# A hybrid linear-attention and softmax-attention encoder: order of the key products, and of the first weight blocks and last input blocks of a feed-forward stage

## The chip, the cores and the metric

One core of one Trainium2 chip runs the whole program in one launch. A core has five engines with an instruction stream each: TensorE (PE: matrix products and transposes, results in PSUM), VectorE (DVE), ScalarE (ACT), GpSimd (POOL) and SyncE (SP, which only starts transfers). They meet through semaphores. Transfers are started from the queue of SP, ACT or POOL and carried out by 16 DMA engines. The metric is the device time of the launch in microseconds (us), the median of several runs. A profile is a trace of one execution; its span runs from the first to the last instruction.

## The reference, cut to what matters

The model has two layers over 528 tokens (512 and 16 learned meta tokens), width 1024, all in float32. A layer is: half a feed-forward step, a mixer, half a feed-forward step.

```python
for l in range(DEPTH):
    h = h + 0.5 * swiglu(rmsnorm(h, g[l, 0]), w_gate[l, 0], w_up[l, 0], w_down[l, 0])
    h = h + mixer(rmsnorm(h, g[l, 1]), ...)
    h = h + 0.5 * swiglu(rmsnorm(h, g[l, 2]), w_gate[l, 1], w_up[l, 1], w_down[l, 1])
return rmsnorm(h, final_norm)[:, N_META:]

def swiglu(x, w_gate, w_up, w_down):                 # hidden width 2816
    return (silu(x @ w_gate) * (x @ w_up)) @ w_down
```

One branch of the mixer is gated linear attention with 4 heads, in chunks and in both directions. For a chunk with decay logs summed up along it (`bcum`, and `btot` at its end) it needs three scaled copies of queries and keys:

```python
q_dec = qc * exp(bcum)            # queries, decayed from the chunk's start
k_inv = kc * exp(-bcum)           # keys for the products inside the chunk
k_end = kc * exp(btot - bcum)     # "end keys": what a key is worth at the chunk's end
att      = where(mask, q_dec @ k_inv.T, 0);   o_intra = att @ vc
kv_chunk = k_end.T @ vc                       # what the chunk adds to the state
```

`k_end.T @ vc` contracts over tokens, so the end keys must be transposed on the chip first. The other branch is softmax attention; the change doesn't touch it.

## The kernel before, in words

**Layout and precision.** Activations lie transposed: 128 channels on the partitions, 528 tokens along the row, eight such chunks for the width. Every large product is done as three products of a rounded high part (`hi`) and the rest (`lo`): hi*hi, hi*lo, lo*hi. A weight tile is 128 x 1024 floats, 512 KB: fetched by SP into `raw` (3 buffers), copied to `whi` by ACT (line 238), and the rest put into `wlo` by DVE (line 239), 4 buffers each. `Weights.use(j)` makes `hi` and `lo` for loads up to j+3 and starts fetches up to j+5 (`AHEAD_MADE`, `AHEAD_FETCHED`).

**A planner sets the order.** The code is traced once. A planner then gives each engine its fixed instruction stream: of the instructions that are ready by its own estimates of durations it takes the one that comes first in the code (`tc.high_priority()` puts some ahead), and it may move a later instruction ahead of one that isn't ready yet. On the chip each stream runs strictly in order, so an instruction that isn't ready in truth holds up all that stands behind it on its engine, also on the queues of SP and POOL.

**Feed-forward stages.** There are four: (0,0), (0,1), (1,0), (1,1), for layer and position. The gate and up products are done for pairs of 128-column blocks (11 pairs a stage) by seven products in place of eight (Strassen-Winograd) on 2 x 2 blocks: the weight is cut in blocks 11, 12, 21, 22, the input in `b11` to `b22` (two channel chunks by two halves of the tokens). Products 1, 2 and 4 take the blocks 11, 12, 22 as fetched. The other four take sums of blocks:

- product 7 takes s3 = 21 - 11 (pool `wsa`, ACT negates 11 on line 189, POOL adds 21)
- product 6 takes s2 = 22 + s3 (pool `wsb`, SP fetches 22, POOL adds s3)
- product 5 takes s1 = 21 + 22 (pool `wsb`, SP fetches 21, POOL adds 22)
- product 3 takes s4 = s2 - 12 (pool `wsa`, ACT negates 12 on line 189, POOL adds s2)

The additions are transfers that add to their target, started from POOL's queue (line 194). `wsa` has 3 buffers and `wsb` has 2. `sums` (lines 196 to 211) is called by `make` just after a block's `hi` and `lo`: for product 1 it does s3 and s2, for product 2 it does s1 and s4.

The input side holds seven combinations for each of four channel pairs, in one tile `xc` with seven slots, `hi` and `lo` (`pair`, lines 475 to 502): slots 0 and 1 are b11 and b21 for products 1 and 2, slots 2 to 5 hold sums for 5, 6, 7, 4, slot 6 is -b22 for product 3. The chunk before the stage calls `chunk_of_pair(c)` as each of the eight chunks of `h` is finished; the sum of squares for the norm is gathered by the way (line 450 on ACT, line 454 on DVE). The norm's factor `rs` itself is only applied later, on the results.

**Openings.** The first products of stages (0,1), (1,0) and (1,1) run while the stage before ends. The order in the code is: products 1 and 2 of pair 0 together (`two_products`, line 580, three channel pairs first and then the last one), products 1 and 2 of pair 1, 6 and 5 of pair 0, 7, 4 and 3 of pair 0, 6 and 5 of pair 1 and so on (line 597). Below, "6 of pair 1" means such a product. Results go through copies of PSUM (`snap`, line 608).

**Linear attention.** `gla_pair` runs per layer for two pairs of heads, each with two directions d, so there are 8 passes. A pass makes the decay logs on ACT (lines 724 to 726), sums them along chunks on DVE (727, 731), subtracts middle and end values (737 to 742), exponentiates on ACT (746 to 755) and forms `qp` on DVE (757), `kp`, the keys inside the chunk, on POOL (758), and `ke`, the end keys, on DVE (760). PE transposes `ke` (764, 765), DVE copies the result out (767, 769). Between these steps PE works on projections of the mixer (line 404, through `project`).

Of the kernel before, what the change touches and what calls it, by code (L numbers as in the profile page):

```python
# [158 lines left out]
class Weights:  # L159
# [35 lines left out]

    def sums(self, f, i, product, w):


        got = self.summed
        if product == "1":  # L200
            s3 = self.negative(f, i, "s3", w)
            self.add(s3, self.dram(f, i, "21"))
            s2 = self.block(f, i, "22", self.short, "wsb")
            self.add(s2, s3)
            got[f, i, "7"], got[f, i, "6"] = s3, s2
        else:
            s1 = self.block(f, i, "21", self.short, "wsb")
            self.add(s1, self.dram(f, i, "22"))
            s4 = self.negative(f, i, "s4", w)
            self.add(s4, got[f, i, "6"])  # L210
            got[f, i, "5"], got[f, i, "3"] = s1, s4

    def fetch(self, upto):

        while self.fetched < min(upto, len(self.loads)):
            load = self.loads[self.fetched]
            if isinstance(load, int):
                w = self.raw.tile([P, SLAB], F32, tag="raw", name=f"raw{load}")
                self.nc.sync.dma_start(w, self.wts[load])
                self.raws[self.fetched] = w  # L220
            elif load[2] in DIRECT:
                self.raws[self.fetched] = self.block(*load[:2], DIRECT[load[2]])
            self.fetched += 1

    def make(self, upto):
        nc = self.nc
        while self.made < min(upto, len(self.loads)):
# [15 lines left out]
            if not isinstance(load, int) and load[2] in ("1", "2"):  # L243
                self.sums(*load, w)
# [28 lines left out]
def build(tc, ctx, xt, wts, win, par, w2, const, umask, out):  # L273
# [10 lines left out]
    slots = {n: pool("s_" + n, b) for n, b in dict(g=16, t=6, rs=2).items()}  # L284
# [151 lines left out]
    class Norm:  # L436
# [38 lines left out]
        def pair(self, j):  # L475
# [18 lines left out]
            S.activation(hi[:, 6], b22, AF.Copy, scale=-1.0)  # L494
            V.scalar_tensor_tensor(lo[:, 6], b22, -1.0, hi[:, 6].bitcast(F32), ALU.mult, ALU.subtract)
# [6 lines left out]
            parts(slice(4, 6), v2(t34))  # L502

# [36 lines left out]
    def ffn(l, f, norm, done, following):  # L540
# [25 lines left out]
        def two_products(p, names):  # L566
# [132 lines left out]
    def gla_pair(l, p, lr, w2t, sr, qa, ka, va, n_out):  # L699
# [17 lines left out]
        for d in range(2):  # L717
# [22 lines left out]
            V.tensor_tensor(a[:, MB], src[:, MB], mm_, ALU.subtract)  # L740
            V.tensor_tensor(blk(ct_), blk(src), tot, ALU.subtract)
            V.tensor_copy(ct_[:, MB], a[:, MB])
            r16 = 1.0 / 16.0
            qp, kp = slot("p"), slot("p")
            if d == 0:
# [3 lines left out]
                S.activation(ct_, ct_, AF.Exp, scale=-r16)  # L749
                ein, eq, ek, eend = c, a, g, ct_  # L750
            else:
                S.activation(c, a, AF.Exp, scale=-r16)
                S.activation(a, a, AF.Exp, scale=r16)
                S.activation(ct_, ct_, AF.Exp, scale=-r16)
                S.activation(g, g, AF.Exp, scale=r16)
                ein, eq, ek, eend = ct_, c, a, g
            V.tensor_tensor(qp[:, :n_out], qa, eq[:, :n_out], ALU.mult)
            G.tensor_tensor(kp, ka, ek, ALU.mult)
            ke = slot("p")
            V.tensor_tensor(ke, ka, eend, ALU.mult)  # L760

            tp = pair()
            for b, bs, _ in blocks:
                TE.transpose(tp[:, 0, bs], ke[:, bs], ident)
            TE.transpose(tp[:META, 1, :P], ke[:, MB], ident)
# [260 lines left out]
    def block_pools():  # L1026
        pools = open_pools("left", wsa=3, wsb=2)
# [248 lines left out]
```

## Time and profile before

| what | value |
|---|---|
| runs | 2263.21 us median of 3 (2260.45 to 2268.38) |
| the profiled execution's own time | 2263.49 us |
| its span | 2261.6 us |
| PE busy | 2204.5 us, 97% of the span |
| DVE, ACT, POOL busy | 1527.2, 1218.3, 164.7 us |
| PE waiting for `ke` at line 764 | 12.5 us in 8 waits |
| additive transfers from POOL | 4 kinds, 43 of each, 512 KB |

On PE the stages lie in the span as follows: (0,0) up to 376 us, mixer of layer 0 to 789, (0,1) to 1148, (1,0) to 1519, mixer of layer 1 to 1900, (1,1) to the end. The page of the profile names each group by line, engine and operation, output and inputs by the program's names: `w<-win` is a block fetched from memory by SP, or added to a `wsb` buffer by POOL; `s<-w` is a `wsa` buffer, either written by ACT from the block it negates (line 189) or raised by POOL by the sum s2 (line 194); `w<-s` is s2 raised by s3; `s<-win` is s3 raised by block 21.

### The profile page before, as it was taken

How to read it: one execution, taken by the hardware profiler on the slowest of the kernel's cores; microseconds unless marked ns; L12 is line 12 of the kernel's file. 1: busy time of each engine (PE TensorE's matmuls, PEld its weight loads, DVE VectorE, ACT ScalarE, POOL GpSimd, SP SyncE). 2: the span in 40 equal slices, each digit the busy share in tenths (PEclk: the TensorE clock that was granted, in tenths of full speed). 3: DMA queues.
4: the chain of work that ended last, by engine and by line, in shares of the span. 5: the costliest groups of instructions: out<-in, count | busy, mean ns of one | idle time of the engine just before them, and what ended most of it. 6: DMA issues, size and time to landing. Idle time of an engine off the chain costs nothing. (4 is left out here: it accounts for less than half of the span.)

```text
span 2261.6 us, 39885 instructions
## 1 busy us (share of the span) xinstructions
PE 2204.5 (97%) x16538; PEld 2102.9 (93%) x16538; DVE 1527.2 (68%) x2397; ACT 1218.3 (54%) x1824; POOL 164.7 (7%) x184
## 2 busy tenths in 40 slices
PE   8999999999999999999979999999999999999998
PEld 8999999989999999999979999998888888989897
DVE  7657567577876666565676565575789767756565
ACT  8536355344784564453565363454557836636354
POOL 1011000000000010101011010100000000101010
PEclk9999999999999999999999999999999999999999
DMA  8778463211113485867658585732121135869661
GB/s 239 188 177 212 134 168 108 75 57 57 48 38 113 124 203 154 197 174 173 180 139 207 139 217 149 178 105 87 56 68 54 47 121 152 215 155 225 156 181 66
DMA packets 87542, 312.85 MB, mean 138 GB/s; under 512 B 9664, under 2 KB 11840, under 8 KB 87360
## 3 DMA queue, kind: packets, MB, share of 16 engines
q1 hardware_dynamic: 60816, 217.67, 28.6%
q0 software_dynamic: 24768, 90.19, 22.5%
q8 instruction: 130, 2.13, 0.4%
q10 hardware_dynamic: 1776, 2.43, 0.3%
q14 instruction: 52, 0.43, 0.1%
HBM read 263.07 MB, written 2.10 MB: 117 GB/s over the span
## 5 line engine op out<-in xcount | busy, mean ns | idle before, releaser
L597 PE MATMUL ss<-xc,whi 128*128 128x264 f32 (+1 forms) x4720 | 865.1, 285 | 16.9 <-ACT whi L238 9.5
L597 PEld LDWEIGHTS ss<-xc,whi 128*128 128x128 f32 x4720 | 734.7, 189 | 19.7 <-ACT whi L238 10.3
L597 PE MATMUL ss<-xc,wlo 128*128 128x264 f32 (+1 forms) x2360 | 671.4, 285 | 5.1 <-DVE wlo L239 5.1
L404 PE MATMUL ss<-g,whi 128*128 128x264 f32 (+1 forms) x2620 | 482.8, 300 | 0.0
L597 PEld LDWEIGHTS ss<-xc,wlo 128*128 128x128 f32 x2360 | 446.8, 189 | 6.4 <-DVE wlo L239 6.3
L404 PEld LDWEIGHTS ss<-g,whi 128*128 128x128 f32 x2620 | 380.6, 188 | 15.7
L404 PE MATMUL mm<-x,whi 128*128 128x264 f32 (+1 forms) x1712 | 385.8, 315 | 0.0
L238 ACT CAST whi<-w 128x1024 fp32r<-128x1024 f32 (+1 forms) x220 | 230.0, 1046 | 266.2 <-PE ss L404 116.1
L239 DVE TENSOR_TENSOR wlo<-w,whi 128x1024 fp32r<-128x1024 f32 (+1 forms) x220 | 266.6, 1218 | 116.1 <-ACT whi L238 114.8
L238 ACT CAST whi<-raw 128x1024 fp32r<-128x1024 f32 x190 | 199.2, 1048 | 260.2 <-PE ss L597 89.8
L239 DVE TENSOR_TENSOR wlo<-raw,whi 128x1024 fp32r<-128x1024 f32 x190 | 232.1, 1222 | 105.8 <-ACT whi L238 104.8
L404 PE MATMUL ss<-g,wlo 128*128 128x264 f32 (+1 forms) x1310 | 302.2, 300 | 0.0
L404 PEld LDWEIGHTS mm<-x,whi 128*128 128x128 f32 x1712 | 281.2, 190 | 15.3 <-DVE x L393 0.2
L404 PE MATMUL mm<-x,wlo 128*128 128x264 f32 (+1 forms) x856 | 265.2, 314 | 0.0
L404 PEld LDWEIGHTS ss<-g,wlo 128*128 128x128 f32 x1310 | 209.2, 188 | 8.3
L239 DVE TENSOR_TENSOR wlo<-s,whi 128x1024 fp32r<-128x1024 f32 x86 | 105.1, 1222 | 95.7 <-ACT whi L238 95.6
L238 ACT CAST whi<-s 128x1024 fp32r<-128x1024 f32 x86 | 90.3, 1050 | 146.9 <-PE ss L597 128.3
L404 PEld LDWEIGHTS mm<-x,wlo 128*128 128x128 f32 x856 | 161.2, 190 | 7.6
L527 DVE SCALAR_TENSOR_TENSOR t<-ss,rs 128x528 f32<-128x528 f32 (+1 forms) x93 | 64.6, 700 | 126.4 <-PE ss L404 126.3
L189 ACT ACTIVATE s<-w 128x1024 f32<-128x1024 f32 x86 | 91.2, 1060 | 81.7 <-DMA w<-win 46.5
L194 POOL DMA_DIRECT2D w<-win x43 | 37.8, 880 | 599.3 <-DVE wlo L239 222.3
L393 DVE TENSOR_TENSOR g<-c,g 128x528 fp32r<-128x528 f32 (+1 forms) x88 | 61.5, 699 | 22.6 <-ACT g L392 22.6
(280 smaller groups left out, 2829.6 us busy)
## 6 DMA issues: line engine op xcount, KB each, us to landing
w<-win SPq DMA_DIRECT2D x218, 512.0 KB, 4.7
raw<-wts SPq DMA_DIRECT2D x190, 512.0 KB, 3.3
w<-win POOLq DMA_DIRECT2D x43, 512.0 KB, 6.8
s<-win POOLq DMA_DIRECT2D x43, 512.0 KB, 6.7
w<-s POOLq DMA_DIRECT2D x43, 512.0 KB, 5.9
s<-w POOLq DMA_DIRECT2D x43, 512.0 KB, 7.0
h<-xt SPq DMA_DIRECT2D x3, 528.0 KB, 7.6
out<-h SPq DMA_DIRECT2D x2, 512.0 KB, 2.9
```

What stands on the lines that cost most here:

```text
L189: self.nc.scalar.activation(t, w, AF.Copy, scale=-1.0)
L194: self.nc.gpsimd.dma_start(t, src, accum_op=ALU.add)
L238: nc.scalar.copy(hi[:, cs], w[:, cs])
L239: nc.vector.tensor_tensor(lo[:, cs], w[:, cs], hi[:, cs].bitcast(F32), ALU.subtract)
L393: V.tensor_tensor(lo, src, hi.bitcast(F32), ALU.subtract)
L404: TE.matmul(acc.half[i][:width], lhs, rhs[:, acc.spans[i]], start=first, stop=last)
L527: V.scalar_tensor_tensor(cut(dst[rows]), pv[rows], -0.5 * f, cut(rs[rows]), ALU.mult, ALU.mult)
L597: TE.matmul(acc[:, j], a[:, j, k], b[:, at], start=bool(begin and k == 0 and i == 0), stop=k == len(x) - 1 and i == 2, skip_group_check=no ...
```

## The change

In the linear attention the end keys and their transposes come first in a pass, under high priority, directly from the decay sums; for d = 0 only the difference that they need is formed, and two small steps fall away. `kp` is formed on VectorE instead of GpSimd.

In the openings, for pair 0 of the three later stages, s3, s2 and s1 are called where block 11 is fetched, and s4 where block 12 is fetched, both two loads earlier in the code than before. For pair 1, s3 and the negation for s4 stay at products 1 and 2, but the fetch and addition of s2, and the addition of s2 to s4, are called after `hi` and `lo` of product 6 of pair 0, and s1 after those of product 5 of pair 0. `wsa` gets a fourth buffer. To make room for it `rs` has one buffer instead of two, and the decay weights (`w2`) live in a pool of the mixer.

The last of the four input pairs is written in two parts: `early` fills slots 0 and 1 straight from `h`; `late`, called after the matrix products of `two_products`, fills slots 2 to 6 and adds the squares of the last two chunks. In every pair slot 6 now comes last.

```diff
+    def third(self, f, i, w):
+        s3 = self.summed[f, i, "7"] = self.negative(f, i, "s3", w)
+        self.add(s3, self.dram(f, i, "21"))
+    def second(self, f, i):
+        s2 = self.summed[f, i, "6"] = self.block(f, i, "22", self.short, "wsb")
+        self.add(s2, self.summed[f, i, "7"])
+    def first(self, f, i):
+        s1 = self.summed[f, i, "5"] = self.block(f, i, "21", self.short, "wsb")
+        self.add(s1, self.dram(f, i, "22"))
+    def fourth(self, f, i, w=None):
+        if w is not None:
+            self.summed[f, i, "3"] = self.negative(f, i, "s4", w)
+        if (f, i, "6") in self.summed:
+            self.add(self.summed[f, i, "3"], self.summed[f, i, "6"])
     def sums(self, f, i, product, w):
...
+        opening = f != (0, 0)
+        if product == "1" and not (opening and i == 0):
+            self.third(f, i, w)
+            if not (opening and i == 1):
+                self.second(f, i)
+        elif product == "2" and not (opening and i == 0):
+            if not (opening and i == 1):
+                self.first(f, i)
+            self.fourth(f, i, w)
+        elif product == "6" and opening and i == 0:
+            self.second(f, 1)
+            self.fourth(f, 1)
+        elif product == "5" and opening and i == 0:
+            self.first(f, 1)
     def fetch(self, upto):
...
+                if load[0] != (0, 0) and load[1:] == (0, "1"):
+                    self.third(*load[:2], w)
+                    self.second(*load[:2])
+                    self.first(*load[:2])
+                elif load[0] != (0, 0) and load[1:] == (0, "2"):
+                    self.fourth(*load[:2], w)
     def make(self, upto):
...
-            if not isinstance(load, int) and load[2] in ("1", "2"):
+            if not isinstance(load, int):
                 self.sums(*load, w)
...
-    slots = {n: pool("s_" + n, b) for n, b in dict(g=16, t=6, rs=2).items()}
+    slots = {n: pool("s_" + n, b) for n, b in dict(g=16, t=6, rs=1).items()}
...
+        def early(self, j):
+            hs = slice(0, live[0] // 2)
+            hi, lo = self.seven()
+            self.x.append((hi, lo))
+            for r in range(2):
+                S.activation(hi[:, r], h(2 * j + r, hs), AF.Identity, scale=col(self.gc + 2 * j + r))
+                V.scalar_tensor_tensor(lo[:, r], h(2 * j + r, hs), col(self.gc + 2 * j + r), hi[:, r].bitcast(F32),
+                                       ALU.mult, ALU.subtract)
+        def late(self):
+            self.pair(KC // 2 - 1)
+            for c in (KC - 2, KC - 1):
+                self.square(c)
         def chunk_of_pair(self, c):
-            if c % 2 and c < KC - 1:
+            if c < KC - 2:
                 self.square(c)
-            if c % 2:
+            if c == KC - 1:
+                self.early(c // 2)
+            elif c % 2:
                 self.pair(c // 2)
-            if c == KC - 1 or c % 2 == 0:
-                self.square(c)
...
+            norm.late()
             for name in names:
                 finished(p, name)
...
-            mm_, mt_ = c[:, T - 1 : T].broadcast_to([P, META]), None
+            last = c[:, T - 1 : T].broadcast_to([P, META])
+            r16 = 1.0 / 16.0
+            ke = slot("p")
             src = c
-            if d == 1:
-                V.tensor_tensor(g, c, g, ALU.subtract)
-                src = g
+            with tc.high_priority():
+                if d == 0:
+                    V.tensor_tensor(blk(ct_), blk(c), tot, ALU.subtract)
+                    V.tensor_tensor(ct_[:, MB], c[:, MB], last, ALU.subtract)
+                    S.activation(ke, ct_, AF.Exp, scale=-r16)
+                else:
+                    V.tensor_tensor(g, c, g, ALU.subtract)
+                    S.activation(ke, g, AF.Exp, scale=r16)
+                    src = g
+                V.tensor_tensor(ke, ka, ke, ALU.mult)
+            tp = pair()
+            for b, bs, _ in blocks:
+                TE.transpose(tp[:, 0, bs], ke[:, bs], ident)
+            TE.transpose(tp[:META, 1, :P], ke[:, MB], ident)
...
             V.tensor_tensor(qp[:, :n_out], qa, eq[:, :n_out], ALU.mult)
-            G.tensor_tensor(kp, ka, ek, ALU.mult)
-            ke = slot("p")
-            V.tensor_tensor(ke, ka, eend, ALU.mult)
-
-            tp = pair()
-            for b, bs, _ in blocks:
-                TE.transpose(tp[:, 0, bs], ke[:, bs], ident)
-            TE.transpose(tp[:META, 1, :P], ke[:, MB], ident)
+            V.tensor_tensor(kp, ka, ek, ALU.mult)
...
-        pools = open_pools("left", wsa=3, wsb=2)
+        pools = open_pools("left", wsa=4, wsb=2)
...
-        wt = one.tile([P, 512], F32R, tag="w2", name=nm("w2"))
+        wt = slots["w2"].tile([P, 512], F32R, tag="w2", name=nm("w2"))
...
-        pools = open_pools("left", e=8, i=5, p=7, q=6, k=5, lr=1)
+        pools = open_pools("left", e=8, i=5, p=7, q=6, k=5, lr=1, w2=1)
```

More of the change, by code (lines that the diff above doesn't have):

```diff
@@ L194, in add @@
         self.nc.gpsimd.dma_start(t, src, accum_op=ALU.add)
-    def sums(self, f, i, product, w):
[L199 to L211, printed above, removed]
+    def third(self, f, i, w):
[12 more added lines that the diff above has]
+            self.add(self.summed[f, i, "3"], self.summed[f, i, "6"])
+    def sums(self, f, i, product, w):
+        opening = f != (0, 0)
[12 more added lines that the diff above has]
+            self.first(f, 1)
     def fetch(self, upto):
@@ L221, in fetch @@
             elif load[2] in DIRECT:
-                self.raws[self.fetched] = self.block(*load[:2], DIRECT[load[2]])
+                w = self.raws[self.fetched] = self.block(*load[:2], DIRECT[load[2]])
+                if load[0] != (0, 0) and load[1:] == (0, "1"):
[4 more added lines that the diff above has]
+                    self.fourth(*load[:2], w)
             self.fetched += 1
@@ L502, in pair @@
             parts(slice(4, 6), v2(t34))
+            S.activation(hi[:, 6], b22, AF.Copy, scale=-1.0)
+            V.scalar_tensor_tensor(lo[:, 6], b22, -1.0, hi[:, 6].bitcast(F32), ALU.mult, ALU.subtract)
         def chunk(self, c):
@@ L748, in gla_pair @@
                 S.activation(c, c, AF.Exp, scale=r16)
-                S.activation(ct_, ct_, AF.Exp, scale=-r16)
-                ein, eq, ek, eend = c, a, g, ct_
-            else:
+                ein, eq, ek = c, a, g
+            else:
+                V.tensor_tensor(blk(ct_), blk(src), tot, ALU.subtract)
+                V.tensor_copy(ct_[:, MB], a[:, MB])
                 S.activation(c, a, AF.Exp, scale=-r16)
```

10 lines of the change are left out of this document (2 added, 8 removed).

## The prediction

> **What bounds the kernel now.** I read the page's busy rows first, then the waits of PE, then PE's waits and the granted clock around each opening, then the streams of single engines there. On the page:
>
> ```profile
> span 2261.6 us, 39885 instructions
> ...
> PE 2204.5 (97%) x16538; PEld 2102.9 (93%) x16538; DVE 1527.2 (68%) x2397; ACT 1218.3 (54%) x1824; POOL 164.7 (7%) x184
> ```
>
> PE is the bound nearly everywhere. The change takes no product away, so all it can win is PE's idle time, 2261.6 - 2204.5 = 57.1 us, and the time that PE runs at a lower clock. The waits of PE over the whole span (us in total, times, longest) start with the place that the first part edits:
>
> ```profile
> PE ss L764 <- DVE p L760: 12.5, 8, 2.1
> ```
>
> So the end keys cost 12.5 us, about 1.6 in each of the 8 passes. The same view for the opening of (0,1) alone (788 to 830 us):
>
> ```profile
> PE ss L597 <- DVE wlo L239: 1.3, 2, 0.7
> PE ss L597 <- ACT whi L238: 0.9, 1, 0.9
> ```
>
> of (1,0) (1148 to 1190):
>
> ```profile
> PE ss L597 <- ACT whi L238: 6.9, 2, 4.7
> PE ss L597 <- DVE wlo L239: 2.5, 2, 2.2
> PE ss L597 <- ACT snap L608: 1.7, 1, 1.7
> ```
>
> and of (1,1) (1898 to 1935):
>
> ```profile
> PE ss L597 <- ACT whi L238: 1.6, 1, 1.6
> PE ss L597 <- ACT snap L608: 1.6, 1, 1.6
> PE ss L597 <- DVE wlo L239: 1.3, 2, 0.8
> ```
>
> That is 2.2, 11.1 and 4.5 us: 17.8 for the openings. Idle time has a second price. In the rows of single stretches, PEclk is the granted clock of PE as a share of full speed:
>
> ```profile
> 454.00:460.00 6.00, 6.00 (x35) 5.16 (x33) 3.79 (x10) 0.36 (x1) 0.00 (x0) 0.72 0.29 90
> 491.00:498.00 7.00, 5.33 (x32) 5.29 (x33) 5.28 (x10) 3.58 (x7) 0.00 (x0) 0.76 0.16 64
> 811.00:818.00 7.00, 5.31 (x28) 4.65 (x27) 3.50 (x4) 2.53 (x3) 1.75 (x2) 0.76 0.99 189
> 1178.00:1190.00 12.00, 7.16 (x35) 6.95 (x36) 3.87 (x5) 2.12 (x4) 1.86 (x3) 0.57 0.95 232
> 1920.00:1930.00 10.00, 6.05 (x47) 5.45 (x47) 3.47 (x4) 2.63 (x4) 1.77 (x2) 1.00 0.99 207
> ```
>
> After two passes of linear attention 0.28 of 6 us (454) and 0.24 of 7 (491) are lost, 1.7 us each; in the opening of (0,1) (811) 0.24 of 7, 1.7 again; in (1,0) (1178) 0.43 of 12, 5.2, of which half of the 4.7 us wait, 2.4, fall on time in which PE was idle anyhow; in (1,1) (1920) nothing.
>
> **The change part by part. Linear attention.** POOL's instruction and the DVE instruction that starts just after it, first and last of the eight passes (start, us), and the three groups:
>
> ```profile
> L758 POOL TENSOR_TENSOR p<-i,t x8: 1347/1763/2192, 435.9 to 1640.1; 128x528 f32<-128x528 f32 x8
> L760 DVE TENSOR_TENSOR p<-i,t x8: 696/706/1715, 438.9 to 1641.1; 128x528 f32<-128x528 f32 x8
> L778 DVE COPY dec<-t x16: 148/166/1302, 436.8 to 1643.2; 64x4 f32<-64x4 f32 x16
> ```
>
> ```profile
> 435.88 2.19 POOL L758 TENSOR_TENSOR p<-i,t 128x528 f32<-128x528 f32 x1 [122.50 <-ACT t L746]
> 1640.13 1.73 POOL L758 TENSOR_TENSOR p<-i,t 128x528 f32<-128x528 f32 x1 [12.53 <-ACT t L753]
> ```
>
> ```profile
> 436.79 1.48 DVE L778 COPY dec<-t 64x4 f32<-64x4 f32 x2
> 1641.08 1.34 DVE L760 TENSOR_TENSOR p<-i,t 128x528 f32<-128x528 f32 x1
> ```
>
> Two copies that take 0.33 us together took 1.48 beside POOL (+1.15), a product of 0.70 took 1.34 (+0.64). Each of the 8 passes has one such stretched DVE instruction, it never stands behind line 760 in the stream, and the eight excesses add up to 8.1 us (0.64 to 1.15 each). Since PE waits for line 760 in every pass, 8.1 of the 12.5 us are POOL's doing. The change removes that instruction. It adds one DVE product of 0.70 us a pass, 8 x 0.70 = 5.6 us, but behind the end keys, where PE has projections to run; without that cover it would cost the 5.6. Fewer steps stand before the end keys as well, but the planner will move the transposes up by as much as it reckons the keys come sooner, so I count nothing for that. The rest of the wait, 4.4 us, is what its estimates miss; it can vanish or stay. Of the two clock drops I take one, 1.7 us. Taken: 8.1 + 1.7 = 9.8. Bounds: 0, if the transposes are moved up so far that PE waits as long as now, and 12.5 + 2 x 1.7 = 15.9.
>
> The Trainium skill, page "SBUF — State Buffer", section "SBUF: two separate sides", says that VectorE and GpSimd share a pair of ports as an exclusive lock, held for a whole instruction. By it up to all of GpSimd's 8 x 1.76 = 14.1 us could be blocked and the part would be worth all 12.5 us of wait; the rows show about 1 us of each.
>
> **Openings: sums begun at the fetch.** For pair 0 I cost it at nothing. In (1,1) the negation already runs as soon as the block has landed, long before product 1's own copy:
>
> ```profile
> 1877.69 1.06 ACT L189 ACTIVATE s<-w 128x1024 f32<-128x1024 f32 x1
> 1887.88 1.05 ACT L238 CAST whi<-w 128x1024 fp32r<-128x1024 f32 x1 [1.14 <-PE mm L404]
> ```
>
> What is late are the sums of pair 1. The end of that opening on SP, POOL and ACT:
>
> ```profile
> 1913.53 0.33 SPq L184 DMA_DIRECT2D w<-win  x1
> ```
>
> ```profile
> 1892.08 0.89 POOL L194 DMA_DIRECT2D s<-w  x1 [5.07 <-ACT t L450]
> 1892.64 1.23 POOL L194 DMA_DIRECT2D s<-win  x1
> 1913.55 0.85 POOL L194 DMA_DIRECT2D w<-s  x1 [19.68 <-DVE c L615]
> 1916.21 0.86 POOL L194 DMA_DIRECT2D w<-win  x1 [1.81 <-DVE wlo L239]
> 1922.97 0.88 POOL L194 DMA_DIRECT2D s<-w  x1 [5.90 <-DMA w<-s]
> ```
>
> ```profile
> 1912.45 1.06 ACT L189 ACTIVATE s<-w 128x1024 f32<-128x1024 f32 x1 [1.09 <-DVE wlo L239]
> 1926.29 1.04 ACT L238 CAST whi<-w 128x1024 fp32r<-128x1024 f32 x1 [2.84 <-DMA w<-win]
> ```
>
> s2 and s1 of pair 1 wait for the two `wsb` buffers, which pair 0's products 6 and 5 hold until their `lo` is made. That stays. What goes is in the fourth `wsa` buffer: the negation at 1912.45 had to wait for the third one, and it held block 12 of pair 1 in its `raw` buffer; at its end, 1913.51, SP fetches the next block (1913.53), in the same moment as the two additions start. With the fourth buffer that negation needs only its block, so this fetch moves ahead, out of the additions' way. How long the two take, here and as a median over the page (KB, us to landing):
>
> ```profile
> w<-s POOLq DMA_DIRECT2D x1, 512.0 KB, 8.8
> w<-win POOLq DMA_DIRECT2D x1, 512.0 KB, 10.0
> ```
>
> ```profile
> w<-s POOLq DMA_DIRECT2D x43, 512.0 KB, 5.9
> w<-win POOLq DMA_DIRECT2D x43, 512.0 KB, 6.8
> ```
>
> The excess is 2.9 and 3.2 us, with two plain fetches beside them, of which one goes; I take 2.0 an opening (bounds 0 and 3.2). In (1,1) that is 2.0. In (0,1) it covers the 0.9 and the 0.7 behind it, 1.6, and the clock drop that followed, 1.7: 3.3. In (1,0) 2.0.
>
> **Last input pair in two parts.** As many instructions as before: slots 0 and 1 come from `h` directly instead of from a scaled copy. Slots 2 to 6 and the last two squares now stand behind the first copies of weights. That may bring product 6's copy, and the snapshot that PE awaits for 1.7 us in (1,0), forward; I take half, 0.8 (bounds -1.7 and 1.7). The norm's factor comes later; it has 9 us to spare:
>
> ```profile
> 1175.40 0.71 DVE L434 SCALAR_TENSOR_TENSOR rs<-t,rs 128x528 f32<-128x528 f32 x1
> 1185.21 0.43 DVE L635 SCALAR_TENSOR_TENSOR c<-c,rs 128x264 f32<-128x264 f32 x1
> ```
>
> One `rs` buffer costs nothing: the old factor is last read by the last chunk of `h`, which the new one needs anyhow. `w2` in the mixer's pool is written where the stage before read its input sums, and all of that stage's last down products lie between.
>
> Sum: 9.8 + 3.3 + (2.0 + 0.8) + 2.0 = 17.9. From the profiled execution's own 2263.5 that leaves 2245.6; it stands 0.3 above the median of the runs, so I predict 2245.
>
> By the Trainium skill, page "TensorE: Matmul & The Clock Gate", section "What's actually happening", the clock falls only after an idle window of about 3.4 us. The row at 811 doesn't agree (0.9 and 0.7 us of waiting, and it fell), nor does the one at 1920 (4.5 us in three waits, and it held); by that rule the two clock terms would go and the sum be 17.9 - 3.4 = 14.5.
>
> **The rivals.** *Only the linear attention gains*: the openings hang on the two `wsb` buffers, which stay, and the planner, seeing earlier blocks, puts products forward just as far. 2263.2 - 9.8 = 2253. For it: SP fetches the moment a buffer is free (1913.51 and 1913.53), so whatever isn't bound by contention comes no sooner. Against: the 8.8 and 10.0 above.
>
> *Nothing is won*: the transposes move up and PE waits as before, within 2 or 3 us of 2263. Against: POOL's stretches, which went straight into the waits.
>
> *All of it is won*: 15.9, 3.9 in (0,1), 8.6 in (1,0) (`whi` and `snap`), 3.2 in (1,1), 31.6 together: 2232.
>
> *A wait on POOL's queue in the openings, slower.* In the code the addition of s2 to s4 of pair 1 now stands ahead of the addition to s1, where before it stood behind. It can't start before s2 has landed. If the planner issues it first, s1's addition starts after 1922.97 + 0.88 instead of at 1916.21, 7.6 us later, and product 5 of pair 1, which PE awaits, comes as much later: 7.6 in (1,0) and (1,1) each, half of it in (0,1), 19 us, with clock drops of 1.7 in two of them 22.4; less the 9.8: 2276. It decides from some 3.3 us of delay an opening on. For it: at 1892.08 the planner put just such an addition in front of another (1892.64) and POOL waited 5.07 us for landing, so it reckons additions faster than they are. Against: s1's block lands only 2.7 us behind s2's (1913.55, 1916.21), and an addition would have to be reckoned at less than that.
>
> **How the numbers follow.** Chances: forecast 0.50 (its own range 2237 to 2251), linear attention alone 0.18, all 0.10, nothing 0.10, POOL's queue 0.12. 0.3% is 6.8 us and about what a measurement tells: faster is below 2256.4. Forecast and all count as faster, of the second case 0.15; 0.75. Within 0.3%: nothing, and 0.03 of the second, 0.13. Slower: 0.12. The range runs from the case of all, 2232, to that of nothing, 2263; the slow case is left out.
>
> **What would show it.** Right: no POOL instruction in the mixer, lines of `dec` and `ke` at 0.17 and 0.70 us throughout, PE's wait for the transposes below 5 us in 8; in the openings ACT's negations without a wait for `wlo`, the two additions of pair 1 nearer to 7 us, no clock drop at 811. Wrong: PE waiting 12 us at the transposes again; the order `w<-s`, `s<-w`, `w<-win` on POOL; or new waits of PE on the sums of slots 2 to 6.

## The result and the profile after

The changed kernel takes 2301.07 us (median of 6 runs, 2297.43 to 2305.88), the kernel before beside it 2262.55 us (6 runs): ratio 1.0165, interval 1.0147 to 1.0184. It is slower by 38 us where I forecast 18 us faster, and it lies far above the range that I gave, 2232 to 2263.

The page of the changed kernel: its busy row, the product line (before: line 597, now 638) and the negations of weight blocks (line 189), each with its busy time, mean in ns, and the idle time in front of it with what ended most of it.

```profile
span 2295.6 us, 39826 instructions
...
PE 2215.3 (97%) x16538; PEld 2110.7 (92%) x16538; DVE 1516.1 (66%) x2405; ACT 1215.9 (53%) x1824; POOL 150.7 (7%) x176
...
L638 PE MATMUL ss<-xc,whi 128*128 128x264 f32 (+1 forms) x4720 | 875.8, 287 | 52.9 <-ACT snap L649 46.5
...
L189 ACT ACTIVATE s<-w 128x1024 f32<-128x1024 f32 x86 | 91.0, 1059 | 154.9 <-DMA w<-win 153.9
```

The span grew by 34.0 us. PE has the same 16538 matmuls, yet is busy 10.8 us longer (2215.3 - 2204.5), and idle 23.2 us longer (80.3 against 57.1). Where in the span? The product line alone, in three stretches of each kernel, shows when the gate and up products of the stages begin and end (the two figures after the durations are first and last start, in us; the middle row holds (0,1) and (1,0) together). Before:

```profile
L597 PE MATMUL ss<-xc,whi x1120: 278/284/422, 34.8 to 346.6; 128*128 128x264 f32 x187
L597 PE MATMUL ss<-xc,whi x2400: 278/284/588, 789.1 to 1489.8; 128*128 128x264 f32 x185
L597 PE MATMUL ss<-xc,whi x1200: 275/281/387, 1900.4 to 2219.1; 128*128 128x256 f32 x172
```

After:

```profile
L638 PE MATMUL ss<-xc,whi x1120: 278/284/590, 34.9 to 356.4; 128*128 128x264 f32 x187
L638 PE MATMUL ss<-xc,whi x2400: 278/284/588, 789.2 to 1512.6; 128*128 128x264 f32 x185
L638 PE MATMUL ss<-xc,whi x1200: 275/281/582, 1920.3 to 2253.0; 128*128 128x256 f32 x172
```

| stretch | before, us | after, us | difference |
|---|---|---|---|
| products of (0,0) | 311.8 | 321.5 | +9.7 |
| from there to (0,1): down products, mixer 0 | 442.5 | 432.8 | -9.7 |
| products of (0,1), down products, products of (1,0) | 700.7 | 723.4 | +22.7 |
| down products, mixer 1 | 410.6 | 407.7 | -2.9 |
| products of (1,1) | 318.7 | 332.7 | +14.0 |

So the mixers won 12.6 us, a little more than the 9.8 that I had taken for the linear attention, and the feed-forward products lost 46.4. They lost it in (0,0) as well, where the sums aren't begun at the fetch. The waits of PE over the whole span (us in total, times, longest) give the loss its name. For ScalarE's snapshots before:

```profile
PE ss L597 <- ACT snap L608: 7.4, 4, 3.8
```

After, the snapshots and four other waits:

```profile
PE ss L638 <- ACT snap L649: 46.5, 18, 7.4
PE ss L638 <- ACT xc L539: 2.9, 1, 2.9
PE ss L791 <- DVE t L794: 2.0, 4, 0.6
PE ss L638 <- ACT xc L513: 1.4, 1, 1.4
PE ss L791 <- DVE p L788: 1.3, 4, 0.6
```

The transposes (now line 791) wait 3.3 us where it was 12.5. PE's wait for ScalarE's snapshots of PSUM went from 7.4 us in 4 times to 46.5 in 18. What holds a copy of 0.6 us back? Line 189, the negations that fill the `wsa` buffers, has ScalarE standing idle before it (us, times) until these. Before:

```profile
  DMA w<-win: 46.5, 19
  DVE wlo L239: 35.2, 43
```

After:

```profile
  DMA w<-win: 153.9, 55
  DVE wlo L264: 1.0, 1
```

Before, half of the 86 negations waited for `wlo`, that is for a free `wsa` buffer, 0.8 us each. With a fourth buffer these waits are gone, and 107 us more are spent waiting for the block itself to land. ScalarE's stream at one such place in (0,0), start and duration in us. Before:

```profile
188.64 1.06 ACT L189 ACTIVATE s<-w 128x1024 f32<-128x1024 f32 x1 [0.79 <-DVE wlo L239]
189.60 0.58 ACT L608 COPY snap<-ss 128x528 f32<-128x528 f32 x1
```

After:

```profile
188.81 0.59 ACT L649 COPY snap<-ss 128x528 f32<-128x528 f32 x1
196.19 1.06 ACT L189 ACTIVATE s<-w 128x1024 f32<-128x1024 f32 x1 [6.79 <-DMA w<-win]
197.15 0.58 ACT L649 COPY snap<-ss 128x528 f32<-128x528 f32 x1
```

PE in the changed kernel, right behind it:

```profile
197.78 0.81 PE L638 MATMUL ss<-xc,whi 128*128 128x264 f32 x2 [3.98 <-ACT snap L649]
```

In both kernels a negation stands ahead of a snapshot. Before, the block has landed when the `wsa` buffer comes free, so the snapshot is held up by a microsecond. After, the planner takes a negation of a later block (the 14th of the kernel at this place, before it was the 13th), since a buffer is free, and ScalarE stands before it for 6.79 us until that block lands. The snapshot behind it keeps the PSUM tile `ss` occupied, and PE stands for 3.98 us. (0,1) and (1,1) have the same thing with another instruction in front: the copy of a sum that POOL's addition hasn't finished. ScalarE there:

```profile
809.10 1.06 ACT L189 ACTIVATE s<-w 128x1024 f32<-128x1024 f32 x1
818.59 1.04 ACT L263 CAST whi<-w 128x1024 fp32r<-128x1024 f32 x1 [8.44 <-DMA w<-win]
819.54 0.59 ACT L649 COPY snap<-ss 128x528 f32<-128x528 f32 x1
```

and POOL:

```profile
802.59 0.88 POOL L194 DMA_DIRECT2D w<-s  x1 [20.72 <-DVE wlo L264]
...
808.12 0.86 POOL L194 DMA_DIRECT2D s<-w  x1 [3.08 <-DMA w<-s]
808.74 1.14 POOL L194 DMA_DIRECT2D w<-win  x1
```

That is the order which one of my rivals named: `s<-w` of pair 1 ahead of `w<-win`. So two theories stood at this point, beside the one that the earlier fetches simply crowd the transfers: ScalarE's order with the fourth buffer (all stages), and POOL's order (the openings).

### The profile page after: what moved, and what is told of

Its sections match the earlier page's. It is cut to its first block, busy times and chain, and to the rows that moved or that the text cites. A ratio compares the mean times of both kernels' runs of the same rounds, so it can differ in the third digit from the quotient of the medians.

```text
span 2295.6 us, 39826 instructions
## 1 busy us (share of the span) xinstructions
PE 2215.3 (97%) x16538; PEld 2110.7 (92%) x16538; DVE 1516.1 (66%) x2405; ACT 1215.9 (53%) x1824; POOL 150.7 (7%) x176
## 4 chain that ended last, share of the span: by engine, by line
PE 72%; DMA 10%; DVE 8%; ACT 6%; issue 3%; POOL 0%; SPq 0%; DVEq 0%; ACTq 0%; POOLq 0%
PE ss L429 26%; PE ss L638 23%; PE mm L429 13%; DMA w<-win 8%; DVE wlo L264 3%; PE sm L429 2%; ACT whi L263 2%; PE sm L1020 1%; DMA w<-s 1%; PE ss L995 1%; PE ss L620 1%; ACT snap L649 1%; ACT t L412 1%; PE sm L1036 1%; PE ss L996 1%
## 5 line engine op out<-in xcount | busy, mean ns | idle before, releaser
L638 PE MATMUL ss<-xc,whi 128*128 128x264 f32 (+1 forms) x4720 | 875.8, 287 | 52.9 <-ACT snap L649 46.5
L189 ACT ACTIVATE s<-w 128x1024 f32<-128x1024 f32 x86 | 91.0, 1059 | 154.9 <-DMA w<-win 153.9
L661 DVE TENSOR_TENSOR c<-snap,ss 128x528 f32<-128x528 f32 (+1 forms) x43 | 29.9, 696 | 76.0 <-ACT snap L649 76.0
```

Of the source, the lines that this page charges most:

```text
L189: self.nc.scalar.activation(t, w, AF.Copy, scale=-1.0)
L638: TE.matmul(acc[:, j], a[:, j, k], b[:, at], start=bool(begin and k == 0 and i == 0), stop=k == len(x) - 1 and i == 2, skip_group_check=no ...
L661: V.tensor_tensor(st["c"][:, :, 3], st["r"], st["Z"][:, :, :w], ALU.add)
```

## The experiments

Ratios are to the kernel before, run on the same chip, with their 95% intervals.

**Three buffers.** The changed kernel with one number different:

```diff
-        pools = open_pools("left", wsa=4, wsb=2)
+        pools = open_pools("left", wsa=3, wsb=2)
```

> The changed kernel with three wsa buffers again, all else kept. Theory A (the fourth buffer lets the planner put ACT's negations ahead of the PSUM snapshots, and on the chip they wait there for blocks that have not landed): PE's wait for the snapshots falls from 46.5 us to about 7, and the time to 2250, some 12 below the kernel before, which is what the linear attention won. Theory B (the loss sits in the openings, on POOL's queue): with three buffers the addition to s4 of pair 1 has no place ahead of that to s1, so the openings come back, but the waits between the openings stay: about 2285. Theory C (one rs buffer, or the moved decay weights): nothing comes back, about 2300.

2255.31 us, 0.9951 (0.9936 to 0.9966). The whole loss goes with the buffer. The negations wait 53.9 us for blocks, and PE for snapshots:

```profile
PE ss L638 <- ACT snap L649: 9.7, 3, 4.0
```

**The fourth buffer alone.** The kernel before, with the room made as in the change (one `rs` buffer, `w2` in the mixer's pool), and:

```diff
-        pools = open_pools("left", wsa=3, wsb=2)
+        pools = open_pools("left", wsa=4, wsb=2)
```

> The kernel before with four wsa buffers, one rs buffer and the decay weights in the mixer's pool, and no other part of the change. Theory A: PE's wait for the snapshots goes from 7.4 us to over 35, clock drops of some 10 us come with it, the time is 2300 or a little more, as the gain of the linear attention is missing. Theory B: the order on POOL's queue is that of the kernel before, so 2262. Theory C: 2300 too, but with the waits at the norm's factor or at the first decay product and not at the snapshots.

2319.24 us, 1.0234 (1.0217 to 1.0251). The waits of PE and of the negations in this kernel:

```profile
PE ss L597 <- ACT snap L608: 44.8, 20, 5.7
```

```profile
  DMA w<-win: 162.1, 53
```

These are nearly the two numbers of the changed kernel (46.5 and 153.9). The time is higher than I expected: PE is busy for 2232.0 us, 27.5 longer than before, where I had reckoned with some 10 us of clock drops. Since the kernel with three buffers has the same `rs` and `w2`, these two are not it. The buffer costs 2.1 to 2.3% by itself, in the changed kernel (1.0165 / 0.9951) as in the one before.

**Snapshots on another engine.** If ScalarE's order is the cause, the negations may wait as long as they like, once nothing stands behind them that PE needs. The changed kernel, four buffers and all, with one line different:

```diff
-                S.copy(st[name], acc)
+                V.tensor_copy(st[name], acc)
```

> The changed kernel, four buffers and all, with one line different: the snapshots of products 1, 6 and 7 are copied by VectorE instead of ScalarE. Theory A (a negation that waits on ScalarE for its block's landing holds up the snapshots that stand behind it in ScalarE's stream, and PE waits for the snapshots): the negations wait as long as in the changed kernel (about 150 us in 55 times), but nothing that PE awaits stands behind them; PE's wait for snapshots falls from 46.5 us to below 15, and the time to 2250 to 2265 us. Theory B (the blocks and sums asked for earlier slow the transfers themselves, and PE waits for weights late by that): the waits only change their names, 2290 to 2305. Theory C (the weight copies on ScalarE are held up as well, and PE waits for them once the snapshots no longer hide it): the wait for the copies goes from about 10 to 30 us or more, 2275 to 2295.

2257.47 us, 0.9949 (0.9930 to 0.9969). PE's wait for snapshots and the next largest in this kernel:

```profile
PE ss L638 <- DVE snap L649: 9.2, 8, 2.9
PE ss L638 <- DVE wlo L264: 8.5, 11, 1.8
...
PE ss L638 <- ACT whi L263: 3.4, 3, 2.6
```

The negations, and the same place in (0,0), on ScalarE:

```profile
  DMA w<-win: 156.4, 49
```

```profile
195.75 1.06 ACT L189 ACTIVATE s<-w 128x1024 f32<-128x1024 f32 x1 [6.45 <-DMA w<-win]
```

and VectorE:

```profile
191.55 0.70 DVE L649 COPY snap<-ss 128x528 f32<-128x528 f32 x1
```

ScalarE waits as before, 156.4 us in all and 6.45 here, but the snapshot is taken at 191.55, four microseconds ahead of the negation, and PE doesn't stand. Theory B, that crowded transfers make the weights late for PE, can explain little: the negations' blocks are waited for as long as ever, and PE doesn't wait. In the changed kernel itself a plain 512 KB fetch of a block takes 4.5 us as a median, against 4.7 before; of the four kinds of additions two take longer (7.4 and 7.9 us against 6.8 and 6.7), the other two as long or less. C, that the weight copies are held up as well, has the 3.4 us above for it, and of the wait for low halves what goes beyond the changed kernel's 2.6 us.

The snapshots are still waited for, and the longer of these waits can be followed once: at 819.55 a negation starts after 3.71 us of waiting for its block, behind it stands an activation (line 412, 820.52), for which VectorE waits 2.22 us; VectorE's snapshot comes at 825.62, and PE, idle for 2.42 us, goes on at 826.48. By these rows ScalarE's wait reaches PE there by way of VectorE.

The control is the same line in the kernel before:

```diff
-                S.copy(st[name], acc)
+                V.tensor_copy(st[name], acc)
```

> The kernel before with the same line different (snapshots on VectorE): the control for the run with four buffers. PE's wait for snapshots there is small, so by theory A little can be won; what it may cost is VectorE's longer queue. Theory A: 2255 to 2270. If moving the snapshots wins 30 us or more here too, the run with four buffers says nothing on the buffers.

2257.62 us, 0.9945 (0.9926 to 0.9964), inside what theory A expected. The move wins 0.55% there and 2.1 points with four buffers (1.0165 to 0.9949). So some 1.6 points are the buffer's harm undone. Not all of the harm is undone: the changed kernel with the move has the gain of the linear attention in it, the control has not, and the two take the same time.

**POOL's order.** The changed kernel, with the addition to s4 of pair 1 issued after the one to s1:

```diff
         elif product == "6" and opening and i == 0:
             self.second(f, 1)
-            self.fourth(f, 1)
         elif product == "5" and opening and i == 0:
             self.first(f, 1)
+            self.fourth(f, 1)
```

> The changed kernel, with the addition of s2 to s4 of pair 1 called after that to s1 (behind product 5 instead of 6 of pair 0). On POOL's queue s1 then stands ahead of s4 in all three openings. Theory A: only the openings gain, 7.4 us of wait in (0,1) and 7.0 in (1,1) fall to 2 or 3 each and part of the clock drops goes, 2285 to 2291. Theory B: 2262 or below.

2303.32 us, 1.0155 (1.0122 to 1.0188): no difference from the changed kernel that can be told. In the profiles (this one is of an execution of 2291.07 us; the other three took 2303 to 2309) the longest wait of (0,1) goes from 7.4 to 5.3 us and that of (1,1) from 7.0 to 4.6, some 4.5 us together, while the total wait for snapshots stays at 43.9. My rival was right in its order; its price of 7.6 us an opening was too high.

**Negations behind their block's own copy.** The obvious mend, with four buffers: the calls that make the sums are issued only once ScalarE has copied the same block to `whi`, by which time it has landed.

```diff
-                nc.scalar.copy(hi[:, cs], w[:, cs])
+                copied = nc.scalar.copy(hi[:, cs], w[:, cs]).ins
...
-                self.sums(*load, w)
+                with self.tc.issue_after(copied):
+                    self.sums(*load, w)
```

> The changed kernel with its four wsa buffers, but each negation on ACT is tied behind the copy to hi of the same block, which needs the block anyhow. Theory A (the harm is the place of the negation in ACT's stream): PE's wait for the snapshots falls from 46.5 us to 10 or less, ACT's wait for blocks in front of negations from 154 to some 50, the time to 2250 to 2258. Theory D (the harm is the traffic: with a fourth buffer blocks are fetched earlier and the transfers slow each other): hardly better than the changed kernel, 2290 or more.

2386.98 us, 1.0527 (1.0511 to 1.0543), 86 us above the changed kernel: a miss for theory A, and more than theory D had a reason for. The negations don't wait any more (0.8 us in all), but PE and ScalarE in this kernel wait like this:

```profile
PE ss L640 <- ACT snap L651: 95.8, 31, 7.9
```

```profile
ACT whi L263 <- DMA w<-s: 227.8, 37, 10.2
```

The sums begin later, the copies of s2 (`w<-s`) aren't ready in their turn, and now these stand in front of the snapshots. Is it again only the order, or are late sums what PE misses? The same kernel with the snapshots on VectorE:

```diff
-                S.copy(st[name], acc)
+                V.tensor_copy(st[name], acc)
```

> The kernel with four buffers whose sums are begun only behind the block's own copy, which took 1.0527 of the time before, with the snapshots on VectorE. Leading theory (ScalarE still waits about 230 us, now at the copies of weights, for the late sums, and it was the snapshots behind these copies that PE waited for): ScalarE's wait stays near 230, PE's wait for snapshots falls from 95.8 to below 20 and the time to 1.00 to 1.01 of before. Rival (the late sums themselves are what PE needs): PE waits for the copies or low halves of the weights instead, 60 us or more, and the ratio stays above 1.03.

2302.54 us, 1.0159 (1.0134 to 1.0185). ScalarE, then PE:

```profile
ACT whi L263 <- DMA w<-s: 287.4, 36, 12.7
```

```profile
PE ss L640 <- ACT whi L263: 18.6, 12, 3.7
PE ss L640 <- DVE wlo L264: 14.5, 20, 1.9
```

Neither expectation holds in full. The move takes 3.7 of the 5.3 points, and no wait for snapshots above 0.2 us is left: that much were the snapshots behind a waiting ScalarE, less the half point that the move wins in the kernel before. The other 1.6 remain. PE now waits 33 us for the weights themselves (6 without the move) and 13 us more for ScalarE's and VectorE's halves of the gated results `g` (lines 419 and 420) in front of the down products. Sums that are begun too late cost as well as negations issued too early.

**The end keys alone.** The kernel before with only the linear-attention part of the diff:

```diff
+            with tc.high_priority():
...
+                V.tensor_tensor(ke, ka, ke, ALU.mult)
...
-            G.tensor_tensor(kp, ka, ek, ALU.mult)
+            V.tensor_tensor(kp, ka, ek, ALU.mult)
```

> The kernel before with the linear-attention part alone (end keys and transposes first, kp on VectorE). By the prediction's first step: PE's wait for the transposes falls from 12.5 us to under 4.4, two clock drops of 1.7 us go, the time is 2250 to 2253. The rival (the planner moves the transposes up by as much): 2260 to 2263.

2252.51 us, 0.9935 (0.9919 to 0.9952). PE's wait for the transposes is 3.4 us. Times the ratio of the fourth buffer alone this gives 0.9935 x 1.0234 = 1.0167; the whole change measured 1.0165. That it fits so well is in part luck, since the other parts aren't free, as the runs below show.

**Its two halves.** First the engine of `kp` alone, in the kernel before:

```diff
-            G.tensor_tensor(kp, ka, ek, ALU.mult)
+            V.tensor_tensor(kp, ka, ek, ALU.mult)
```

> The kernel before with nothing but kp on VectorE; the end keys stay behind it. The eight stretched VectorE instructions (8.1 us too much) go, but a product of 0.70 us now stands ahead of the end keys in each pass (5.6 us). If the planner leaves the transposes where they were, PE's wait for them goes from 12.5 to 10; if it sets them later by what it reckons for the product, to 4.4. Time 2255 to 2263.

2253.92 us, 0.9934 (0.9920 to 0.9948), a little better than I expected. PE's wait there:

```profile
PE ss L764 <- DVE p L760: 4.8, 8, 1.0
```

Then the new order with `kp` on GpSimd as before:

```diff
-            V.tensor_tensor(kp, ka, ek, ALU.mult)
+            G.tensor_tensor(kp, ka, ek, ALU.mult)
```

> The linear-attention part with kp on GpSimd as before. By the prediction's reading GpSimd's instruction only harms because it falls in front of the end keys: now it runs behind them, and PE's wait for the transposes is as low as with kp on VectorE (3.4 us), the time 2250 to 2255. If kp on VectorE is what counts: wait 8 or more, 2258 to 2263.

2259.26 us, 0.9964 (0.9948 to 0.9979). Two of its groups on VectorE, and PE's waits for the transposes:

```profile
L780 DVE TENSOR_TENSOR p<-i,t 64x528 f32<-64x528 f32 (+1 forms) x16 | 12.9, 804 | 0.2
L781 DVE COPY dec<-t 64x4 f32<-64x4 f32 x16 | 6.2, 385 | 0.3
```

```profile
PE ss L750 <- DVE p L747: 4.5, 5, 1.3
PE ss L750 <- DVE t L753: 1.6, 3, 0.6
```

The time lies where I expected it if the engine is what counts; the wait, 6.1 us, lies between the two expectations. The change of engine by itself gives all of the gain, the new order by itself about half. With the order and `kp` on VectorE the first of these groups has 11.1 us instead of 12.9, and the product that makes the end keys (line 747) takes at most 0.71 us instead of 1.82: with GpSimd the stretching remains and falls on other instructions, once on the end keys themselves.

**The last input pair in two parts.** The end keys, and of the openings only `early` and `late` (with slot 6 last in every pair):

```diff
+            if c == KC - 1:
+                self.early(c // 2)
...
+            norm.late()
```

> The kernel before with the linear-attention part and the last input pair in two parts; weight sums and buffers as before. It tells what is behind the 2.8 us by which the changed kernel with three buffers stood above the linear attention alone (ratios 0.9951 and 0.9935). If it is the two parts (PE waits 1.4 and 2.9 us for the input sums of lines 513 and 539 in the opening of (1,0)): ratio 0.995, 2255. If it is the sums begun at the fetch: 0.9935, 2251. By the prediction's step (a gain of 0.8): below 0.9935.

2255.53 us, 0.9945 (0.9932 to 0.9957), against 0.9935 without the two parts. PE waits:

```profile
PE ss L613 <- ACT snap L624: 11.2, 3, 4.1
...
PE ss L613 <- ACT xc L514: 2.9, 1, 2.9
```

The 2.9 us wait for an input is new, another 1.4 comes beside it, and the snapshots are waited for twice as long as with the end keys alone (5.6). The span of this profile, of an execution of 2258.04 us where the other four took 2253.56 to 2256.43, is 5.5 us longer than that of the end keys alone (2256.2 and 2250.7). By the ratios it is 0.1 points, some 2 us, and the intervals overlap: the time alone doesn't show a loss here.

**Sums begun at the fetch, three buffers.** The end keys with the new `sums` and `fetch`, the input in one part:

```diff
+                if load[0] != (0, 0) and load[1:] == (0, "1"):
+                    self.third(*load[:2], w)
+                    self.second(*load[:2])
+                    self.first(*load[:2])
```

> The linear-attention part with the sums begun at the fetch, three buffers, and the last input pair in one part as before (the kernel with three buffers less the two parts). Theory: the sums begun at the fetch are worth nothing when the buffers are three, and the two parts cost 2 to 3 us: 2249 to 2256, the same as the end keys alone (2252.5). Rival (they win in the openings what the prediction took, 1.3 to 3 us an opening, and the two parts ate it): 2243 to 2248.

2250.36 us, 0.9914 (0.9893 to 0.9935). Against the end keys alone (0.9935) the intervals overlap, and the spans are 2248.5 and 2250.7: at most 2 us, no more than one wait can differ between two runs. The three-buffer kernel above (0.9951) differs in the two parts, and also in the place of slot 6, in one `rs` buffer for two and in the pool of `w2`; all this together costs 6.8 us of span, 0.37 points by the ratios, whose intervals just part (0.9935 and 0.9936). The two parts have new waits of PE to account for it, the others weren't tried by themselves.

**The gains together.** That kernel with the snapshots on VectorE:

```diff
-                S.copy(st[name], acc)
+                V.tensor_copy(st[name], acc)
```

> End keys first and key products on VectorE, sums begun at the fetch, three buffers, the last input pair in one part, and the snapshots on VectorE: the two gains that the runs have shown, put together. Theory: they lie at different places and add: 0.9914 x 0.9945 = 0.986, with PE's wait for snapshots (6.5 us without the move) gone and the transposes' wait at 3.3. Rival (VectorE, which now has the key products and the snapshots, makes the low halves of the weights late, and PE waits for these instead): 0.991 or above, with PE's wait for the low halves up from 5 to 10 us or more.

2243.72 us, 0.9898 (0.9878 to 0.9918). It is faster than the kernel before with the move alone (0.9945); against 0.9914 the intervals overlap. The two gains don't quite add: 0.986 lies below the interval. No wait for snapshots is left among PE's waits (6.5 us before the move), and the one for ScalarE's copies falls from 9.3 us, but VectorE's low halves are later: 5.1 us before the move, now

```profile
PE ss L622 <- DVE wlo L264: 8.0, 9, 2.2
...
PE ss L622 <- ACT whi L263: 6.6, 6, 3.1
```

## Why the prediction was wrong, step by step

**Linear attention: right.** I took 8.1 us of the 12.5 for POOL's doing; the change of engine alone took the wait from 12.5 to 4.8, that is 7.7. I counted nothing for the order, and beside the change of engine it brings nothing that can be measured (0.9935 and 0.9934). By itself the order does count: with GpSimd's product kept, the wait fell to 6.1 us. The total was too small: 9.8 taken, 12.6 won in the stretches of the mixers.

The exclusive lock of the Trainium skill ("SBUF — State Buffer", SBUF: two separate sides) agrees with the trace before: each of the eight stretched VectorE instructions ends 0.03 to 0.57 us after the GpSimd product beside it. The estimate that the prediction made with it, that all of the 12.5 us might go, isn't borne out: 4.8 us stayed when no GpSimd product was left, and 3.4 when the keys were moved ahead as well.

**Openings, sums begun at the fetch: the step that failed.** It reads: "With the fourth buffer that negation needs only its block, so this fetch moves ahead, out of the additions' way", priced at 2.0 us an opening with bounds 0 and 3.2. The first half is true, and it is the fault. A negation that needs only its block is put into ScalarE's stream as soon as the planner believes the block there, and it believes too early. I had read the negation's wait for `wlo` (1.09 us at 1912.45) as a cost to be taken away, and named its absence as a sign of being right; the sign came (1.0 us in one wait) and the time went up, because that wait was what kept the negation behind its block's landing. In its place came 107 us more of ScalarE waiting for blocks and 39 us more of PE waiting for snapshots. I asked what the buffer lets start sooner on SP, and not what would then stand behind it on ScalarE, and I looked at pair 1 of three openings for a pool that serves all 11 pairs of four stages. The lower bound of zero had no reason behind it that excluded a loss. The excess that the step priced was also read too simply: of the two additions only the one at 1913.55 starts with the fetch, the other 2.7 us later.

What the step promised did come in part. In (1,1) the two additions of pair 1 landed after 5.2 and 9.1 us instead of 8.8 and 10.0; whether the moved fetch did it isn't shown, as the second now starts 6.2 us after the first instead of 2.7. In (1,0), by PE's waits there, the wait for copies of weights is 1.1 us instead of 6.9 (with three buffers its longest is still 6.0). In (0,1) and (1,1) the waits for snapshots took more than that back: 7.4 and 7.0 us, where the openings had 2.2 and 4.5 in all.

**Two parts: no gain, and probably wrong in sign.** 0.8 us taken, with a bound of -1.7. The two comparisons have it cost 5.5 and 6.8 us of span, some 2 and 8 us by the ratios, the first of them not apart from nothing and the second with other small differences in it. I had looked for new waits on slots 2 to 6. The new waits of the changed kernel are on the first parts of the inputs, 2.9 us for what `early` writes (line 539) and 1.4 us for the third pair (line 513), both in (1,0) and in place of a wait of 2.2 us for `wlo`; and the waits for snapshots grew. Why these grew hasn't been tried.

**The rivals.** The slower one (2276) had the right engine order on POOL and named the wrong queue as the one that decides: putting it right changed PE's longest waits in two openings by 4.5 us and the time by nothing measurable. None of the others had a loss in it. "Only the linear attention gains" (2253) is what three buffers give (2255.31).

**The clock terms.** I took 1.7 us a drop, and the profile after shows more of them. Stretches of 7 us of the changed kernel right behind a wait of PE; the figure after the busy times is PEclk, the granted clock. The waits in front of the first three rows are 3.98 us (the row at 197.78 above), 7.4 and 2.9 us (the last 2.0 us after one of 1.4), in front of the last two 1.3 and 1.2 us:

```profile
197.80:204.80 7.00, 7.00 (x38) 7.00 (x39) 4.94 (x7) 3.41 (x4) 0.69 (x1) 0.63 0.47 136
...
820.20:827.20 7.00, 7.00 (x43) 7.00 (x44) 3.22 (x5) 2.11 (x2) 0.86 (x1) 0.71 0.62 150
...
1175.10:1182.10 7.00, 6.96 (x44) 6.96 (x45) 5.91 (x13) 4.35 (x9) 0.00 (x0) 0.76 0.01 2
...
842.40:849.40 7.00, 6.99 (x57) 6.99 (x58) 6.93 (x11) 4.52 (x6) 0.67 (x1) 1.00 0.43 135
...
2076.40:2083.40 7.00, 6.97 (x59) 6.97 (x60) 6.92 (x11) 4.67 (x6) 0.54 (x1) 1.00 0.44 138
```

Behind the long waits 0.24 to 0.37 of 7 us are lost, 1.7 to 2.6 us each; behind the short ones nothing. Part of the 10.8 us by which PE is longer busy lies there: the stall of 4 us costs 6.6. The idle window of about 3.4 us that the Trainium skill gives ("TensorE: Matmul & The Clock Gate", What's actually happening) can't be one unbroken wait in these traces either: the clock fell behind the wait of 2.9 us too, and in the kernel before behind single waits of 2.1 and 1.8 us (the rows of the prediction at 454 and 491), while one of 2.2 us (1150) left it at 1.00. What decides isn't shown. (The prediction's "4.5 us in three waits" at 1920 are four; the row itself holds three, 3.95 us.)

What stays open: with the snapshots on VectorE the changed kernel (0.9949) is still 0.5 points, some 11 us, behind the version with three buffers and the input in one part (0.9898). Between 2 and 8 us of that go with the two parts and the small differences beside them. For the rest the traces name one place: PE waits 9.2 us for VectorE's snapshots in the one and not at all in the other, once by the way followed above. No run takes it away by itself.

## What to carry to other kernels

Before giving a pool another buffer, ask which instruction will be issued earlier because of it, what it will wait for instead, and what stands behind it on its in-order engine: here a wait of 0.8 us for a buffer, at half of the negations, was the throttle, and without it ScalarE stood 107 us more in front of data still on its way. Keep the short copies that free PSUM for PE off an engine whose stream has instructions waiting for transfers; in this kernel moving them took 2.1 points off the changed kernel and 0.55 where there was no such harm. And a bound of zero on a change needs its own reason: look at every place that the resource serves, not only at the one for which it was added.

## What the runs showed of the hardware that I had not expected

Behind stalls of PE of 2.9 to 7.4 us the granted clock over the next 7 us was 0.63 to 0.76, so that a stall of 4 us cost 6.6; behind stalls of 1.2 and 1.3 us it stayed at 1.00, and between 1.8 and 2.2 us it went either way. And moving one GpSimd product of about 1.8 us in each of 8 passes to VectorE, with nothing else changed, made the kernel 0.66% faster (0.9934, some 15 us of the 2268.8 us that the kernel before took beside it), about twice the 7.7 us by which PE's wait at the transposes fell. In the two profiled executions, both at a granted clock of 0.992, the spans differ by only 8.3 us. The other half goes with the clock: seven of the eleven executions of the kernel before in that comparison had 0.988 or 0.989 (spans of 2265.9 to 2269.1 us), all four with `kp` on VectorE 0.992 to 0.994. Why that many had the lower clock no row shows.
